# First S5 stage of a four-layer trunk: angle products moved behind the outputs on TensorE, their clips moved on VectorE

## The chip, the cores and the metric

The kernel runs on one core of a Trainium2 chip. A core has a matrix engine (TensorE, PE in the profile; its weight loads are PEld), a vector engine (DVE), a scalar engine (ACT), GpSimd (POOL) and a queue engine (SP) that here only issues DMAs. Each engine takes its own list of instructions strictly in order and waits on semaphores for the others. The metric is the device time of one execution in microseconds; the time before is the median of three runs.

## The reference, cut to what matters

The reference is a trunk of four layers over 512 tokens of width 1024 in fp32: an S5 mixer, a gated linear attention, a differential attention and again an S5 mixer, each followed by a SwiGLU network. The change lies in the first S5 mixer. Its state is complex and diagonal; the powers of the diagonal are needed as magnitudes and as cosines and sines of angles:

```python
ab_mag = jnp.exp(lr * dt)
ab_ang = li * dt
...
p_mag = jnp.exp(lr * dt * j)
p_ang = li * dt * j
p_re = p_mag * jnp.cos(p_ang)
p_im = p_mag * jnp.sin(p_ang)
...
y = jnp.einsum('bcgp,ghp->bcgh', s_re, cr) - jnp.einsum('bcgp,ghp->bcgh', s_im, ci)
...
y = y + d_skip.astype(f32) * h.astype(f32)
z = jax.nn.gelu(y).astype(h.dtype)
a, b = jnp.split(z @ w_glu, 2, axis=-1)
return a * jax.nn.sigmoid(b)
```

The mixer's 64 groups times 64 states are worked through in eight blocks of 512 columns (four state tiles of 128 rows by 128 positions; four tokens are folded into one position).

## The kernel before, in words

`s5_first` runs the first S5 mixer through `s5_pipe`, a loop over ten steps `kk` in which block `kk` has its states made, block `kk - 1` its outputs, and block `kk - 2` its share of the GLU product. The order of instructions on every engine is the order in which this Python code issues them: `hand_all()` switches the automatic scheduler off for the stage, and `s5_first` hangs its own pieces of work into the loop by named hooks (`first`, `behind states`, `operators`, `ahead of zp`, `behind products`, `behind scans`, `beside`). A hook is called at one place of the step, and whatever it issues stands there in the lists of all engines. Behind the stage the scheduler works again.

One step of the loop, in order: hook `first`; six DVE operations that turn the products `V` back by cosine and sine (`states`, L1383 to L1388); hook `behind states`; the outputs of the block before, on PE (`outputs`, tile `y`, L1412 and L1414, then the gelu on ACT, L1416); hook `operators`; the transposition of the inputs two blocks ahead (`up`, L1357, copied by ACT, L1370); hook `ahead of zp`; the transposition of the gelu's result (`zp`, L1429, copied by ACT, L1430); the products `V` of the next block (L1378); hook `behind products`; two scans on DVE (L1392); hook `behind scans`; four multiplications on DVE that turn the scanned states forward (`turn`, L1401 and L1405, into `prods`); hook `beside`; the low half of the gelu's result on DVE (`rest`, L1434); the GLU products (L370 to L372).

The angles of a block come in four pieces (`s5_phases_first`):

- `rough` (L1003, L1004): two PE products over 12 rows give the number of turns, and ACT rounds it in two operations (`turns` L1005, `turnsr` L1007).
- `angle` (L1011 to L1013): three PE products into one PSUM bank; the second takes the whole turns off and so waits for `turnsr`.
- `clip` (L1016): one DVE operation from that bank into the block's table `cs`.
- `sines` (L1019 to L1021): three ACT operations in `cs`. Sine and gelu need different function tables, so ACT loads a table when it changes between them.

`rough` and `angle` take their banks from one group of four (tag `acc`), which the GLU uses later; a bank comes free when its reader (ACT for `rough`, DVE for `angle`) is done. `y`, `up`, `zp`, `xps`, `cps` and `rps` share two banks (tag `tp`).

Other pieces that stand near the change: `new_q` (PE `cps` L1089, ACT copies L1110) and the two halves of `Q` on DVE (L1043 to L1045) make the output operators of two blocks; `out_pads` copies them into place by DMA (`scr<-Q`, L1135, SP's queue). `s5_rows` (PE `rps`, L1145) and `s5_map` make the direct map of two blocks: DVE (L1155) and ACT (L1159) write `rsb`, a DMA takes it to DRAM (`rd<-rsb`, L1161), and eight DMAs, four each on SP and POOL, bring it back in another shape (`scr<-rd`, L1170). The outputs read that map. `ins` makes the input operators (PE `xps` L1179, ACT L1202). `decays` copies the decay on ACT (L1029), and POOL clears its first columns (L1030). Weights of the GLU are split into high and low halves (ACT L346, DVE L350).

Of the kernel before, what the change touches and what calls it, by code (L numbers as in the profile page):

```python
# [268 lines left out]
class Trunk:  # L269
# [1257 lines left out]
    def s5_first(self, ctx):  # L1527
# [5 lines left out]
        with self.tc.tile_pool(name="s5_0", bufs=1) as p:  # L1533
# [24 lines left out]
            def new_x(h):  # L1558
                X[h] = self.s5_x(nc.vector, p, 0, 8 * h, 8, raw[h][0], 2, gain)
                X[h][1]()  # L1560

            def new_q(h):
                Q[h] = self.s5_q(nc.vector, p, 0, 8 * h, 8, 2)
                Q[h][1](self.s5_qt(raw[h][1]))
# [27 lines left out]
            def phases(*pieces):  # L1592
                for kk, name in pieces:
                    if name == "rough":
                        ph[kk] = self.s5_phases_first(kk, cs(kk))
                    ph[kk][name]()

            def decays(kk):
                r4[kk] = p.tile([P, 512], F32, tag="r4", name="r4", bufs=2)
                self.s5_decays(0, kk, r4[kk][:])  # L1600

            def ins(kk):
                self.s5_inms(inm[kk % 2], self.s5_xts(X[kk // 2][0], 4 * (kk % 2)))

            def out_pads(kk):
                self.s5_out_pads(oms[kk % 2], Q[kk // 2][0], slice(4 * (kk % 2), 4 * (kk % 2) + 4))
# [19 lines left out]
                raw[2] = self.s5_loads(p, 0, 16, 8, 2)  # L1626

            def first(kk):
                if kk == 1:
                    phases((5, "angle"))  # L1630
                if kk == 2:
                    raw[3] = self.s5_loads(p, 0, 24, 8, 2)
                if 1 <= kk < 7:
                    decays(kk + 1)

            def behind_states(kk):
                if kk == 0:
                    phases((1, "clip"))
                    self.s5_map(0, 0, 8, rv[0], rs, mops[0])

            def operators(kk):
                if kk in (2, 4, 6):
                    h = kk // 2
                    rv[h] = self.s5_rows(8, bp, Q[h][0])
                    if h > 1:
                        self.s5_map(0, 8 * h, 8, rv[h], rs, mops[h % 2])
                if 1 <= kk < 7:
                    ins(kk + 1)
# [5 lines left out]
            def behind_products(kk):  # L1654
                if kk == 0:
                    phases((3, "angle"), (4, "rough"))
                if kk == 1:
                    phases((6, "rough"), (7, "rough"), (6, "angle"))
                if kk == 2:
                    phases((7, "angle"))  # L1660
                if kk == 3:
                    phases((4, "sines"), (5, "sines"), (6, "sines"), (7, "sines"))
                if kk % 2 == 0 and 2 <= kk < 7:
                    out_pads(kk + 1)

            def behind_scans(kk):
                if kk == 0:
                    phases((2, "clip"), (2, "sines"), (4, "angle"), (5, "rough"))
                if kk == 1:
                    phases((4, "clip"), (5, "clip"))  # L1670
                if kk == 2:
                    self.s5_map(0, 8, 8, rv[1], rs, mops[1])
                    phases((6, "clip"))

            def beside(kk):
                h = kk // 2
                if kk == 2:
                    phases((7, "clip"))
                if kk % 2 == 0 and kk < 6:
                    if kk:  # L1680
                        new_x(h + 1)
                        X[h + 1][2]()
                    X[h + 1][3]()
                    self.s5_b_pads(bp, X[h + 1][0])
                if kk % 2 == 0 and kk < 6:
                    new_q(h + 1)
                if kk == 0:
                    phases((3, "clip"), (3, "sines"))
                if kk % 2 and kk < 7:
                    Q[h + 1][2]()  # L1690
                    Q[h + 1][3]()
                    out_pads(kk + 1)

            rv = {}
            hooks = {
                "first": first, "operators": operators, "behind states": behind_states, "ahead of zp": ahead_of_zp,
                "behind products": behind_products, "behind scans": behind_scans, "beside": beside,
            }
            accs = self.s5_pipe(0, hu, zT, True, room, get, before, hooks)
# [726 lines left out]
```

## Time and profile before

| | before |
|---|---|
| median of three runs | 2325.21 us (2324.91 to 2325.57) |
| profiled execution | 2320.61 us, span 2318.9 us |
| granted TensorE clock, mean | 0.989 |
| PE busy | 2221.3 us, 96% of the span |
| DVE busy | 1593.3 us, 69% |
| ACT busy | 1112.6 us, 48% |
| POOL busy | 284.5 us, 12% |

A row of the timeline has the start and the length in us, the engine, the line of the kernel, the operation, the tile written and the tiles read, and in brackets the idle time of the engine before it with what ended it. SPq is a DMA issue on SP's queue; its length is that of issuing, not of the transfer. A row of a window has the stretch, its length, the busy time of PE, PEld, DVE, ACT and POOL with the number of instructions, then the granted clock of TensorE (1.00 is full speed), the busy share of the DMA engines and GB/s.

### The profile page before, as it was taken

The page shows a single profiled execution, that of the slowest core. Times are in us where ns is not written, and L with a number is a line of the kernel's source. Part 1 is how long each engine was busy: PE and PEld are TensorE (multiplying, and loading weights), DVE is VectorE, ACT ScalarE, POOL GpSimd, SP SyncE. Part 2 cuts the span into 40 slices and gives each one's busy share as a digit, 9 for nine tenths or more (in the row PEclk, how much of TensorE's full clock was granted, in tenths as well). Part 3 has the DMA queues.
Part 4 walks back from the last instruction along what each step waited for, and adds up shares of the span by engine and source line. Part 5 has one row for each costly group of instructions (what it writes and reads, how often), then busy time and mean ns, then how long its engine had stood idle before and what let it go on. Part 6 is the DMA issues. An engine that isn't in the chain of part 4 may idle for free. (4 is left out here: it accounts for less than half of the span.)

```text
span 2318.9 us, 37158 instructions
## 1 busy us (share of the span) xinstructions
PE 2221.3 (96%) x14847; PEld 1969.5 (85%) x14847; DVE 1593.3 (69%) x2461; ACT 1112.6 (48%) x1769; POOL 284.5 (12%) x394
## 2 busy tenths in 40 slices
PE   5899999999999999999999999999999899999997
PEld 3788979898877789898988887899999788989996
DVE  8784877786624578776744675976766965967674
ACT  5533645454453355555535675654534224635342
POOL 1000141522000010101002131110000100101000
PEclk8999999999999999999999999999999999999999
DMA  4156567663422457575336365876641555766531
GB/s 85 37 141 171 138 166 183 169 175 97 129 73 73 133 138 196 155 191 156 100 124 151 91 150 143 216 206 152 171 96 46 140 158 151 191 161 161 160 81 64
DMA packets 293927, 319.91 MB, mean 138 GB/s; under 512 B 70077, under 2 KB 233177, under 8 KB 293498
## 3 DMA queue, kind: packets, MB, share of 16 engines
q1 hardware_dynamic: 231130, 235.79, 33.9%
q0 software_dynamic: 62624, 81.75, 19.1%
q8 instruction: 117, 1.92, 0.3%
q14 instruction: 56, 0.46, 0.1%
HBM read 285.62 MB, written 16.65 MB: 130 GB/s over the span
## 5 line engine op out<-in xcount | busy, mean ns | idle before, releaser
L350 DVE TENSOR_TENSOR whl<-wst,whl 128x1024 fp32r<-128x1024 f32 x272 | 331.9, 1223 | 280.6 <-ACT whl L346 279.8
L346 ACT CAST whl<-wst 128x1024 fp32r<-128x1024 f32 x272 | 285.6, 1052 | 382.8 <-PE acc L372 259.8
L535 PE MATMUL a<-side,whl 128*128 128x256 f32 x3168 | 384.9, 278 | 10.0 <-ACT whl L346 5.9
L535 PEld LDWEIGHTS a<-side,whl 128*128 128x128 f32 x3168 | 371.7, 189 | 12.5 <-ACT whl L346 7.2
L370 PE MATMUL acc<-whl,act 128*128 128x512 f32 x704 | 278.0, 395 | 1.2 <-DVE g L580 0.8
L371 PE MATMUL acc<-whl,act 128*128 128x512 f32 x704 | 274.9, 391 | 0.0
L372 PE MATMUL acc<-whl,act 128*128 128x512 f32 x704 | 274.7, 390 | 0.0
L535 PE MATMUL c<-side,whl 128*128 128x256 f32 x2112 | 255.6, 277 | 5.8 <-DVE whl L350 5.8
L535 PEld LDWEIGHTS c<-side,whl 128*128 128x128 f32 x2112 | 248.1, 189 | 6.6 <-DVE whl L350 6.6
L350 DVE TENSOR_TENSOR whl<-slot,whl 128x1024 fp32r<-128x1024 f32 x105 | 127.9, 1223 | 65.7 <-ACT whl L346 65.1
L370 PEld LDWEIGHTS acc<-whl,act 128*128 128x128 f32 x704 | 132.1, 188 | 30.8 <-DVE g L580 1.2
L372 PEld LDWEIGHTS acc<-whl,act 128*128 128x128 f32 x704 | 132.2, 188 | 27.8
L371 PEld LDWEIGHTS acc<-whl,act 128*128 128x128 f32 x704 | 132.2, 188 | 26.0 <-issue 0.2
L346 ACT CAST whl<-slot 128x1024 fp32r<-128x1024 f32 x105 | 110.1, 1054 | 73.9 <-PE acc L372 28.1
L370 PE MATMUL acc<-whl,hT 128*128 128x512 f32 x352 | 142.9, 406 | 2.1 <-DVE ro L2151 1.5
L371 PE MATMUL acc<-whl,hT 128*128 128x512 f32 x352 | 137.9, 392 | 1.0 <-DVE whl L350 1.0
L372 PE MATMUL acc<-whl,hT 128*128 128x512 f32 x352 | 137.9, 392 | 0.0
L535 PE MATMUL a<-sides,whl 128*128 128x256 f32 x1056 | 134.0, 283 | 1.6 <-DVE x L518 1.6
L535 PE MATMUL d<-sides,whl 128*128 128x256 f32 x1056 | 133.4, 283 | 1.3 <-ACT whl L346 1.3
L535 PEld LDWEIGHTS a<-sides,whl 128*128 128x128 f32 x1056 | 129.5, 191 | 2.7 <-issue 2.0
L535 PEld LDWEIGHTS d<-sides,whl 128*128 128x128 f32 x1056 | 128.9, 191 | 1.9 <-ACT whl L346 1.9
L571 POOL DMA_DIRECT2D wst<-in_ffn_w_gate_up_dram x44 | 57.1, 1297 | 436.5 <-DMA wst<-in_ffn_w_gate_up_dram 239.1
(449 smaller groups left out, 3909.1 us busy)
## 6 DMA issues: line engine op xcount, KB each, us to landing
wst<-in_ffn_w_gate_up_dram SPq DMA_DIRECT2D x88, 512.0 KB, 4.7
wst<-in_ffn_w_down_dram SPq DMA_DIRECT2D x88, 512.0 KB, 4.5
slot<-in_ffn_w_gate_up_dram SPq DMA_DIRECT2D x69, 512.0 KB, 5.5
wst<-in_ffn_w_gate_up_dram POOLq DMA_DIRECT2D x44, 512.0 KB, 6.2
halves<-in_ffn_w_gate_up_dram SPq DMA_DIRECT2D x42, 512.0 KB, 5.7
wst<-in_s_w_glu_dram SPq DMA_DIRECT2D x32, 512.0 KB, 4.5
wst<-in_gla_w_in_dram SPq DMA_DIRECT2D x24, 512.0 KB, 3.7
wst<-in_diff_w_qkv_dram SPq DMA_DIRECT2D x24, 512.0 KB, 3.7
```

The lines of the kernel that those rows point to most:

```text
L346: self.last["high"] = self.nc.scalar.copy(hl[:, 0], w[:])
L350: self.last["low"] = self.nc.vector.tensor_tensor(hl[:, 1], w[:], hl[:, 0].bitcast(F32), op=ALU.subtract)
L370: mm(out, lh, rh, start=first, stop=False)
L371: mm(out, lh, rl, start=False, stop=False)
L372: self.last["mm"] = mm(out, ll, rh, start=False, stop=last)
L535: mm(o, hl[:, x, k, c], side[:, y, k], start=first and not (j or k or n), stop=k == 3 and n == 2, skip_group_check=True,)
L571: nc.gpsimd.dma_start(w[:], left.quarter(*plus, b), accum_op=ALU.add)
```

## The change

Only the places of `angle`, `clip` and `sines` of blocks 3 to 7 in the hooks of the first S5 stage differ. No instruction is added or removed.

- Angle 4 was issued behind the scans of step 0, and angle 5 at the start of step 1. Both now stand in `operators` of step 1, behind the outputs of block 0 on PE.
- Angle 6 stood behind the products of step 1 (ahead of the outputs of block 1), and angle 7 behind the products of step 2. Both now stand in `operators` of step 2, behind the outputs of block 1 and ahead of `s5_rows`.
- Clip 3 and sines 3 were in `beside` of step 0. They are now in `behind states` of step 1: on DVE behind the six operations of step 1's states, on ACT behind the decay of block 2.
- Clips 4 and 5 were behind the scans of step 1. They are now in `beside` of step 1, behind the four turns and ahead of `Q`.
- Clips 6 and 7 and sines 4 to 7 stay where they are.

In the built program PE's list differs by these moves of three products each, DVE's by the three clips, ACT's by one swap (the decay copy of block 2 ahead of sines 3), and SP's list is the same; on POOL two clears of decays are in the same places and write other buffers.

```diff
--- before.py
+++ after.py
@@ -1626,8 +1626,6 @@
                 raw[2] = self.s5_loads(p, 0, 16, 8, 2)
 
             def first(kk):
-                if kk == 1:
-                    phases((5, "angle"))
                 if kk == 2:
                     raw[3] = self.s5_loads(p, 0, 24, 8, 2)
                 if 1 <= kk < 7:
@@ -1637,8 +1635,14 @@
                 if kk == 0:
                     phases((1, "clip"))
                     self.s5_map(0, 0, 8, rv[0], rs, mops[0])
+                if kk == 1:
+                    phases((3, "clip"), (3, "sines"))
 
             def operators(kk):
+                if kk == 1:
+                    phases((4, "angle"), (5, "angle"))
+                if kk == 2:
+                    phases((6, "angle"), (7, "angle"))
                 if kk in (2, 4, 6):
                     h = kk // 2
                     rv[h] = self.s5_rows(8, bp, Q[h][0])
@@ -1655,9 +1659,7 @@
                 if kk == 0:
                     phases((3, "angle"), (4, "rough"))
                 if kk == 1:
-                    phases((6, "rough"), (7, "rough"), (6, "angle"))
-                if kk == 2:
-                    phases((7, "angle"))
+                    phases((6, "rough"), (7, "rough"))
                 if kk == 3:
                     phases((4, "sines"), (5, "sines"), (6, "sines"), (7, "sines"))
                 if kk % 2 == 0 and 2 <= kk < 7:
@@ -1665,9 +1667,7 @@
 
             def behind_scans(kk):
                 if kk == 0:
-                    phases((2, "clip"), (2, "sines"), (4, "angle"), (5, "rough"))
-                if kk == 1:
-                    phases((4, "clip"), (5, "clip"))
+                    phases((2, "clip"), (2, "sines"), (5, "rough"))
                 if kk == 2:
                     self.s5_map(0, 8, 8, rv[1], rs, mops[1])
                     phases((6, "clip"))
@@ -1684,8 +1684,8 @@
                     self.s5_b_pads(bp, X[h + 1][0])
                 if kk % 2 == 0 and kk < 6:
                     new_q(h + 1)
-                if kk == 0:
-                    phases((3, "clip"), (3, "sines"))
+                if kk == 1:
+                    phases((4, "clip"), (5, "clip"))
                 if kk % 2 and kk < 7:
                     Q[h + 1][2]()
                     Q[h + 1][3]()
```

## Prediction

> **What bounds the kernel now.** The page comes first: one core, TensorE (PE) busy nearly throughout, so only stretches in which PE waits or runs at a low clock can give time back.
>
> ```profile
> span 2318.9 us, 37158 instructions
> PE 2221.3 (96%) x14847; PEld 1969.5 (85%) x14847; DVE 1593.3 (69%) x2461; ACT 1112.6 (48%) x1769; POOL 284.5 (12%) x394
> ```
>
> The edit lies in steps 0 to 2 of the first S5 stage. Second, the PE timeline of that place. The reader is to see two waits for ACT's `turnsr`, each ahead of outputs (`y`) that need no angle, and one wait for a DMA.
>
> ```profile
> 51.72 0.62 PE L1003 MATMUL rough<-counts,frow 12*128 12x512 f32 x1
> 52.57 0.62 PE L1011 MATMUL angle<-counts,frow 12*128 12x512 f32 x1
> 54.30 0.79 PE L1012 MATMUL angle<-turnsr,nident 128*128 128x512 f32 x1 [1.11 <-ACT turnsr L1007]
> 55.62 0.62 PE L1003 MATMUL rough<-counts,frow 12*128 12x512 f32 x1
> 58.51 0.79 PE L1011 MATMUL angle<-counts,frow 12*128 12x512 f32 x1
> 60.67 0.80 PE L1412 MATMUL y<-scr,room 128*128 128x128 f32 x2
> 62.97 0.63 PE L1412 MATMUL y<-scr,room 128*128 128x128 f32 x2
> 66.08 0.39 PE L1412 MATMUL y<-scr,room 128*128 128x128 f32 x2
> 67.29 1.15 PE L1179 MATMUL xps<-ident,X 64*64 64x64 f32 x32
> 74.34 0.49 PE L1012 MATMUL angle<-turnsr,nident 128*128 128x512 f32 x1 [0.84 <-ACT turnsr L1007]
> 81.43 0.69 PE L1145 MATMUL rps<-Q,bpad 128*32 128x64 f32 x32
> 82.19 1.15 PE L1179 MATMUL xps<-ident,X 64*64 64x64 f32 x32
> 88.32 0.50 PE L1011 MATMUL angle<-counts,frow 12*128 12x512 f32 x1
> 89.59 1.09 PE L1089 MATMUL cps<-ident,craw 128*64 128x128 f32 x16
> 94.47 0.46 PE L1412 MATMUL y<-scr,room 128*128 128x128 f32 x2 [0.84 <-DMA scr<-rd]
> 99.10 1.15 PE L1179 MATMUL xps<-ident,X 64*64 64x64 f32 x32
> 115.14 1.30 PE L1179 MATMUL xps<-ident,X 64*64 64x64 f32 x32 [3.32 <-ACT z L1416]
> ```
>
> Third, the same place in windows (busy time of PE, PEld, DVE, ACT, POOL, then granted clock). The clock changes at multiples of 3.41 us: half speed from 44.32 to 64.80 (six stretches) and again at 75.04 and at 116.00 (one each).
>
> ```profile
> 44.32:61.39 17.07, 15.96 (x52) 10.29 (x52) 13.20 (x21) 11.14 (x22) 2.46 (x5) 0.50 0.31 62
> 61.39:64.80 3.41, 3.41 (x18) 3.41 (x17) 3.41 (x7) 2.09 (x3) 0.11 (x1) 0.50 0.00 0
> 64.80:68.21 3.41, 3.41 (x53) 3.29 (x53) 2.86 (x5) 0.60 (x1) 0.00 (x0) 1.00 0.00 0
> 71.63:75.04 3.41, 2.57 (x12) 1.53 (x10) 3.41 (x6) 2.13 (x4) 0.00 (x0) 1.00 0.37 58
> 75.04:78.45 3.41, 3.41 (x16) 3.19 (x16) 3.00 (x4) 2.03 (x3) 0.10 (x1) 0.50 0.02 5
> 81.87:85.28 3.41, 2.06 (x53) 1.52 (x43) 3.05 (x7) 1.43 (x3) 0.00 (x0) 1.00 0.37 77
> 112.59:116.00 3.41, 0.86 (x28) 0.86 (x30) 3.41 (x6) 2.60 (x5) 0.11 (x1) 1.00 0.00 0
> 116.00:119.41 3.41, 3.17 (x22) 2.66 (x19) 3.41 (x6) 2.29 (x4) 1.76 (x4) 0.50 0.32 72
> 115.14:170.10 54.96, 50.97 (x452) 45.39 (x452) 47.26 (x72) 19.38 (x30) 5.19 (x11) 0.97 0.47 129
> ```
>
> What decides here is the clock. One block of outputs takes 62.97 − 60.67 = 2.30 us slow and 67.29 − 66.08 = 1.21 (with the step to `xps`) fast, so a slow stretch of 3.41 us full of work costs about half of it, 1.71. The stretch that brought the clock back, 61.39 to 64.80, holds outputs alone. What went before it mixed in `rough` and `angle`, products over 12 of 128 rows. The stretch of `rough` and `angle` at 71.63 cost the clock again. I read this as: 12-row products count for little, outputs for full.
>
> **The change, part by part.** *Angles 4 and 5 behind the first outputs.* PE's order becomes rough 4, rough 5, `cps`, outputs 0, angles 4 and 5. Ahead of the outputs go 55.62 − 52.57 = 3.05 us (angle 4 with its wait) and 60.67 − 58.51 = 2.16 (angle 5), so outputs 0 start at 60.67 − 5.21 = 55.46, if their map is there by then. Its DMAs are these:
>
> ```profile
> 46.41 1.76 SPq L1170 DMA_DIRECT2D scr<-rd  x4
> 46.70 2.35 POOL L1170 DMA_DIRECT2D scr<-rd  x4 [2.13 <-DMA rd<-rsb]
> ```
>
> Two steps later the same DMAs, issued from 89.66 on (below), let PE go at 94.47, 4.81 us after; from 46.70 that gives 51.5, four before they are needed. The angles' own work is done later, so 1.11 of the 3.05, the wait, is gain by itself.
>
> *Angles 6 and 7 behind the second outputs.* The wait of 0.84 goes. Angle 7, 89.59 − 88.32 = 1.27, moves from behind the products of step 3 to ahead of `rps` (81.43), where more hangs on it.
>
> *What hangs on `rps`.* It feeds a map that goes through DVE, ACT and two DMAs before outputs 2 may start:
>
> ```profile
> 87.51 0.30 ACT L1159 COPY rsb<-rps 128x96 f32<-128x96 f32 x1
> 87.83 0.37 SPq L1161 DMA_DIRECT2D rd<-rsb  x1
> 89.66 2.99 SPq L1170 DMA_DIRECT2D scr<-rd  x4
> ```
>
> That is 94.47 − 81.43 = 13.04 us, all behind `rps`, and PE waits at its end. So outputs 2 move by what `rps` moves, no more. The 1.27 taken from between them is no gain there. From outputs 2, ACT's chain (copy, sines 4 to 7, gelu) leads to `xps` at 115.14, and PE is then busy 50.97 of 54.96 us: the shift passes on to the end of the stage. Behind it the instruction order is unchanged, and I let the shift pass in full.
>
> *Sum without the clock:* −1.11 − 0.84 + 1.27 = −0.68.
>
> *The clock.* Outputs 0 at half speed from 55.46 fill all of 57.97 to 61.39 and 2.51 of the 3.41 us before it, the rest of which is `cps` (64 columns, no 12-row product). The trace has no stretch of just that mix. From the one that returned on outputs alone, the return is at 61.39 at the latest, one slow stretch less (−1.71); if `cps` counts, at 57.97, two less (−3.41). I take two, since 116.00 to 119.41, made of `xps`, `up` and `zp` beside products, also brought the clock back. The second slow stretch should go: roughs 6 and 7 are followed at once by outputs 1, and the 0.84 of idling is gone (−1.71; other bound 0). The third, after 3.32 us of idling that stays, I keep (bound −1.71). Clock: −5.12.
>
> *Clips on DVE and their cover.*
>
> ```profile
> 51.95 0.69 DVE L1016 TENSOR_SCALAR cs<-angle 128x512 f32<-128x512 f32 x1 [2.13 <-PE angle L1013]
> 60.78 0.69 DVE L1016 TENSOR_SCALAR cs<-angle 128x512 f32<-128x512 f32 x1 [1.71 <-PE angle L1013]
> 63.78 0.68 DVE L1043 TENSOR_TENSOR Q<-Q,pw 128x512 f32<-128x512 f32 x1
> 67.03 0.69 DVE L1045 TENSOR_TENSOR Q<-Q,dq 128x512 f32<-128x512 f32 x1
> 89.69 0.69 DVE L1016 TENSOR_SCALAR cs<-angle 128x512 f32<-128x512 f32 x1 [4.11 <-PE angle L1013]
> ```
>
> Clip 3 goes behind the states of step 1, so its 2.13 vanishes. Clips 4 and 5 now wait for angles behind outputs 0, and `Q` is queued behind them: outputs 0 end near 61.4 (55.46 + 2.30 + 3 × 1.21), two angles at 1.27 each end near 63.9, a clip takes 0.69, and `Q` (63.78 to 67.72, 3.94 long) ends near 68.5 in place of 67.7. Its first reader is `rps`, near 76 then, so it costs nothing; at a slow clock `Q` ends near 71, still covered. Without that cover it would cost up to 3.5. Clip 7's 4.11 goes as angle 7 moves up, and everything DVE does behind 89.69 can start earlier; that is needed, as otherwise DVE would hold the gain back.
>
> *ACT, SP, POOL.*
>
> ```profile
> 61.59 0.60 ACT L1029 COPY r<-s5r 128x512 f32<-128x512 f32 x1
> 62.21 1.28 ACT L1416 ACT_TABLE_LOAD   x1
> ```
>
> The decay copy passes the three sines of block 3, and POOL's memset follows it: the same work in another order, done by 62.21 + 1.28 = 63.49 at the latest. Gelu 0, whose outputs end near 61.4, can thus be 2.1 late; PE has two angles (2.54) and `xps` (1.15) between, which hide it. If they did not, 2.1 is the price. No DMA is reordered on SP or POOL; bounds 0 and 0.84, the longest DMA wait above.
>
> **Sum:** −0.68 − 5.12 = −5.80 against the profiled execution's 2320.61 (span 2318.9 and 1.7 around it): 2314.8. The runs' median is 2325.21, 4.6 above it, so the forecast is 2319.4.
>
> **Rivals.** *The clock returns when it does now.* Only −0.68 remains, or −2.4 with one stretch less: 2324.5 to 2322.8. For it: five of the six stretches after 44.32 held much PE work and stayed slow. Against it: none of those held outputs alone. [...]
>
> *Slower: the clock falls later and stays down.* Angles 6 and 7, `rps`, the narrow `xps`, and the wait for ACT before `up` come in one piece behind outputs 1. For it: that piece looks like 71.63 to 75.04. Against: 81.87 to 85.28 holds most of it, 2.06 busy, and stayed fast. [...] Three more slow stretches (5.1) eat up the clock's gain; from four on it is slower.
>
> *More than forecast:* the third stretch goes too: −7.5, 2317.7.
>
> **How the numbers follow.** 0.2% is 4.65 us, about what a measurement of this kernel can tell from no change. Forecast 0.47, more 0.13: both below 2320.6, faster 0.60. Clock as now, or one stretch: 0.25, same. Slower 0.15. The gate's 3.41 us grid can fall otherwise by one stretch either way, and idle stretches later in the kernel can catch or miss one (1.71 each): so the low end is two stretches under the case of more, 2317.7 − 3.42 = 2314.3, and the high end, leaving out the slower rival, is the median less 0.68 and one stretch more, 2326.2. The forecast's own range is 2317.5 to 2321.
>
> **What would show it.** Outputs 0 near 55.5; granted clock 1.00 from 58 or 61.4, and none at half between 71 and 82; no wait of `angle` for `turnsr`; clip 7 on DVE without its 4.11; outputs 2 near 89 and the `xps` behind gelu near 109. Wrong: 0.50 from 78 on, a PE wait for `Q` at `rps`, or the shift gone by 170.

## The result and the profile after

The changed kernel takes 2318.88 us (median of seven executions, 2312.34 to 2323.66) against 2325.67 us before (seven, 2324.91 to 2332.58): a ratio of 0.9964, with a 95% interval of 0.9951 to 0.9977, some 8.4 us. The ratios here are not quotients of the medians, which lie 6.8 us apart. The forecast was 2319.4.

The profiled execution after took 2318.88 us, its span 2317.2. That is only 1.7 us less than the profiled span before (2318.9), because most of what this profile wins in the stage of the change is lost again behind it. The timeline of TensorE (PE) after, in the stage of the change:

```profile
55.07 0.80 PE L1412 MATMUL y<-scr,room 128*128 128x128 f32 x2
57.37 0.51 PE L1412 MATMUL y<-scr,room 128*128 128x128 f32 x2
58.60 0.39 PE L1412 MATMUL y<-scr,room 128*128 128x128 f32 x2
60.93 0.50 PE L1011 MATMUL angle<-counts,frow 12*128 12x512 f32 x1
61.36 0.49 PE L1012 MATMUL angle<-turnsr,nident 128*128 128x512 f32 x1
69.20 0.49 PE L1412 MATMUL y<-scr,room 128*128 128x128 f32 x2
76.23 0.69 PE L1145 MATMUL rps<-Q,bpad 128*32 128x64 f32 x32
79.28 0.66 PE L1357 MATMUL up<-ident,scr 128*128 128x128 f32 x4 [1.27 <-ACT inm L1202]
88.81 0.46 PE L1412 MATMUL y<-scr,room 128*128 128x128 f32 x2 [0.20 <-issue]
109.46 1.97 PE L1179 MATMUL xps<-ident,X 64*64 64x64 f32 x32 [3.30 <-ACT z L1416]
```

Outputs 0, 1 and 2 start at 55.07, 69.20 and 88.81 (before: 60.67, 75.26, 94.47), each some 6 us sooner. Of the 5.60 at outputs 0, 0.38 was there before anything that was moved: `rough` of block 3 starts at 44.60, against 44.98. Angles 4 and 5 no longer wait for `turnsr`. The first quarter of outputs 0 still takes 2.30 us, the second 1.23: the clock came back at 57.60, just behind the start of the second. The windows of the same trace show the clock (PE, PEld, DVE, ACT, POOL busy, then the granted clock):

```profile
43.95:57.60 13.65, 13.65 (x55) 10.46 (x55) 13.62 (x22) 8.93 (x18) 2.46 (x5) 0.50 0.36 78
57.60:81.50 23.90, 21.27 (x218) 17.00 (x218) 18.26 (x30) 14.23 (x23) 0.21 (x2) 1.00 0.19 34
78.09:81.50 3.41, 1.55 (x12) 1.31 (x13) 3.34 (x7) 1.91 (x4) 0.00 (x0) 1.00 0.00 0
81.50:84.91 3.41, 3.41 (x20) 3.19 (x21) 3.31 (x10) 0.96 (x2) 0.32 (x1) 0.50 0.14 38
105.40:108.81 3.41, 0.76 (x34) 0.53 (x32) 1.80 (x4) 3.38 (x5) 0.10 (x1) 1.00 0.00 0
108.81:115.64 6.83, 5.94 (x50) 5.42 (x51) 6.73 (x15) 3.56 (x6) 2.09 (x4) 0.50 0.35 76
170.00:2300.00 2130.00, 2083.30 (x13706) 1856.58 (x13705) 1442.19 (x2133) 1019.87 (x1619) 264.43 (x346) 0.99 0.54 142
272.64:276.05 3.41, 3.37 (x16) 3.37 (x17) 3.41 (x5) 1.78 (x2) 1.32 (x1) 0.50 0.65 208
```

The long half-speed stretch has become four stretches of 3.41 us, from six. The second did not go away: it moved from 75.04 to 81.50, behind 3.41 us in which PE was busy 1.55. The third became two stretches. The first gate of the GLU on ACT (L1780), which stands at the end of the stage, shows what is left of it all. The row of before, then that of after:

```profile
170.37 2.05 ACT L1780 ACTIVATE gate<-acc 128x512 f32<-128x512 f32 x4
```

```profile
165.25 2.05 ACT L1780 ACTIVATE gate<-acc 128x512 f32<-128x512 f32 x4
```

The stage is 5.12 us shorter, the 0.38 included. Behind it, where the lists of instructions are the same, the profiled execution after was at half speed for 27.30 us, the one before for 17.06. The window from 170 to 2300 shows it as a granted clock of 0.99, against 1.00 before:

```profile
170.00:2300.00 2130.00, 2082.56 (x13717) 1854.92 (x13716) 1443.93 (x2133) 1024.66 (x1625) 264.82 (x346) 1.00 0.55 143
272.64:276.05 3.41, 1.97 (x18) 1.77 (x16) 3.03 (x3) 0.93 (x2) 0.00 (x0) 1.00 0.80 230
```

One of the additional stretches is 272.64 to 276.05, fast before and slow after. On ACT, where the same operations can be set side by side, the lead falls from 5.15 to 3.93 us there and is 1.72 at the end: 3.4 of the 5.12 us are lost again in this pair. That these stretches took them is read from where the lead falls; no run holds them fixed. Over all executions the gain stands.

### The profile page after: what moved, and what is told of

The parts are those of the page before. It is cut to its first block, busy times and chain, and to the rows that moved or that the text cites. A ratio compares the mean times of both kernels' runs of the same rounds, so it can differ in the third digit from the quotient of the medians.

```text
span 2317.2 us, 37158 instructions
## 1 busy us (share of the span) xinstructions
PE 2223.4 (96%) x14847; PEld 1972.9 (85%) x14847; DVE 1593.3 (69%) x2461; ACT 1111.1 (48%) x1769; POOL 284.4 (12%) x394
```

## Experiments

Two theories run through the expectations. One says that the gain is the clock's: products over 12 of 128 rows count for little in what the clock goes by, outputs for full (Theory C). The rival (Theory O) says that it is the order's: waits and work taken off the path by the moves themselves. Each experiment is told with its profile's first gate, and with the half-speed time in the stage.

### Each half of the change alone

The first kernel moves angles 4 and 5 with their clips, and leaves block 3's clip and angles 6 and 7 as they were:

```diff
             def first(kk):
-                if kk == 1:
-                    phases((5, "angle"))
...
             def operators(kk):
+                if kk == 1:
+                    phases((4, "angle"), (5, "angle"))
...
-                    phases((2, "clip"), (2, "sines"), (4, "angle"), (5, "rough"))
-                if kk == 1:
-                    phases((4, "clip"), (5, "clip"))
+                    phases((2, "clip"), (2, "sines"), (5, "rough"))
...
                     phases((3, "clip"), (3, "sines"))
+                if kk == 1:
+                    phases((4, "clip"), (5, "clip"))
```

> Only angles 4 and 5 (with their clips) move; angle 6 stays ahead of the outputs of block 1, angle 7 behind the products, clip 3 in its old place. Stage end read at the first GLU gate on ACT (L1780; 170.4 us before, 165.3 after). Theory C (the gain is mostly the TensorE clock coming back sooner): outputs 0 start near 55, the clock is back at 1.00 by 58 to 61.4 in place of 64.8, gate at 165.5 to 167.5, total 2.5 to 5 us under before. Theory O (the gain is the waits that go, the clock only accompanies): outputs 0 start near 55 too, but the gate comes 1.1 us sooner than before (169.3), total 1.1 under.

The second moves angles 6 and 7 alone:

```diff
             def operators(kk):
+                if kk == 2:
+                    phases((6, "angle"), (7, "angle"))
...
-                    phases((6, "rough"), (7, "rough"), (6, "angle"))
-                if kk == 2:
-                    phases((7, "angle"))
+                    phases((6, "rough"), (7, "rough"))
```

> Only angles 6 and 7 move behind the outputs of block 1. Theory C: outputs 0 at 60.7 and the clock back at 64.8 as before, the half-speed stretch at 75.0 to 78.5 gone, rps at 81.43 + 1.27 - 0.84 - 1.71 = 80.2, gate near 169.1, total about 1.3 us under before; if a stretch of half speed comes behind 78 in its place, no gain or 0.4 slower. Theory O: rps at 81.9, gate 0.4 us later than before (170.8).

Angles 4 and 5 alone: 2325.97 us against 2330.01 before on the same chip, ratio 0.9973 (0.9959 to 0.9987), about −6.3 us. Angles 6 and 7 alone: 2326.37, ratio 0.9990 (0.9977 to 1.0003), about −2.3 us and not told from nothing. The two add up to the whole, −8.6 against −8.4. The ratios put the larger part on angles 4 and 5, but their intervals overlap and the two medians lie 0.4 us apart, so this isn't shown. The PE timeline with angles 4 and 5 moved:

```profile
55.38 0.80 PE L1412 MATMUL y<-scr,room 128*128 128x128 f32 x2
70.42 0.50 PE L1012 MATMUL angle<-turnsr,nident 128*128 128x512 f32 x1 [0.84 <-ACT turnsr L1007]
90.67 0.46 PE L1412 MATMUL y<-scr,room 128*128 128x128 f32 x2 [0.95 <-DMA scr<-rd]
```

Outputs 0 start where they start in the whole change, the clock is back at 57.41 (half speed from 43.76 for 13.65 us), and the wait of angle 6 for `turnsr` is still there, followed by a half-speed stretch at 71.07. The gate comes at 166.19, with 20.48 us at half speed. With angles 6 and 7 alone the gate came at 166.16, with 27.31 us at half speed, but that profile says little on its edit. The clock was fast there from 48.24 to 51.65 and outputs 0 started at 57.46 (60.7 was expected), ahead of anything that the edit touches. The same list of instructions can thus meet the clock in different ways, which is why the next runs change the clock's cause itself.

### The same order with products over 128 rows

If products over 12 rows keep the clock low, they should not when all 128 rows are driven. This edit gives the operands of `rough` and `angle` 128 rows, of which rows 12 to 127 are zeros. The products have the same values, and PE has the same number of instructions; POOL gets two more, which clear the tiles. The edit was made in the kernel before and in the changed kernel:

```diff
-        self.frow = cp.tile([12, 8, P], F32R, name="frow")
+        self.frow = cp.tile([P, 8, P], F32R, name="frow"); nc.gpsimd.memset(self.frow[:].bitcast(F32), 0.0)
...
-        self.counts = cp.tile([12, 2, 4, P], F32R, name="counts")
+        self.counts = cp.tile([P, 2, 4, P], F32R, name="counts"); nc.gpsimd.memset(self.counts[:].bitcast(F32), 0.0)
...
-                self.counts[:, z], y[:12].unsqueeze(2).broadcast_to([12, 4, P]),
+                self.counts[:12, z], y[:12].unsqueeze(2).broadcast_to([12, 4, P]),
...
-            nc.scalar.copy(self.frow[:, 4 * q : 4 * q + 4], ps[:12])
+            nc.scalar.copy(self.frow[:12, 4 * q : 4 * q + 4], ps[:12])
```

> The kernel before, with the two 12-row operands of rough and angle widened to 128 rows, rows 12 to 127 zero: same instructions, same values, 128 rows of TensorE in use where 12 were. Theory C in my reading (12-row products count for little towards the clock): the half-speed time between 44 and 79 us shrinks from 23.9 to under 12, gate at 160 to 166, total 4 to 10 us under before, with no change of order at all. If the clock counts the time that products stream and not their rows, or if rows of zeros don't count: half speed from 44.3 to 64.8 and at 75 as before, gate within 1 us of 170.4. Theory O: total unchanged whatever the clock does.

> The changed kernel with the same 128-row operands. If the widening lifts the clock in both, what is left between this and the widened kernel before is the order alone: -0.7 us (waits of 1.11 and 0.84 gone, angle 7 of 1.27 ahead of rps), gate 0.5 to 1.5 sooner than with the order of before. If the order itself is worth the gain (Theory O): 5 us sooner. If the widening does nothing: gate at 165.3 as after.

Both were run a second time on another chip:

> Second look at the order of before with the clock mostly up. Over the looks so far the gate is 153.9 + 0.55 us per us of half speed in the stage; by that 153.9 plus its own slow time, plus 1 to 2 for the order of before. Gate 157 to 163; ratio 0.993 to 0.997.

> Second look at the changed order with the clock mostly up. Theory C: at equal slow time in the stage 0.7 to 1.6 us ahead of e10, outputs 1 about 3 ahead, outputs 2 about 0.7 to 1.7 ahead, the total not to be told from e10. Theory O: gate 5 us ahead of e10 at equal slow time.

| | first time | second time | first gate, us |
|---|---|---|---|
| order of before, 128 rows | 0.9945 (0.9925 to 0.9965) | 0.9950 (0.9933 to 0.9966) | 161.25, 155.73 |
| changed order, 128 rows | 0.9949 (0.9933 to 0.9965) | 0.9950 (0.9933 to 0.9967) | 161.51, 156.06 |

The order of before with 128 rows gains some 12 us, by the ratios more than the change itself, though the intervals overlap. With it the change adds nothing that the totals can tell, and the lead of 0.5 to 1.5 us that was expected at the gate did not come. The gate of the second order of before, 155.73, is earlier than expected (157 to 163). The windows of the second time, order of before:

```profile
40.00:72.00 32.00, 26.27 (x268) 22.49 (x267) 31.90 (x51) 24.20 (x41) 2.67 (x7) 1.00 0.34 65
72.00:107.00 35.00, 28.61 (x283) 25.31 (x282) 32.15 (x58) 21.52 (x35) 4.41 (x10) 0.95 0.23 48
```

and those of the changed order:

```profile
40.00:72.00 32.00, 26.81 (x276) 23.33 (x275) 31.90 (x51) 24.71 (x41) 2.69 (x7) 1.00 0.34 64
72.00:107.00 35.00, 30.36 (x278) 27.41 (x277) 33.33 (x61) 20.92 (x34) 4.40 (x10) 0.85 0.26 53
```

From 40 to 72 the granted clock is 1.00 in both, and in the first pair too, where before it was 0.50 from 44.32 to 64.80. PE is busy a smaller share of the time (26.3 of 32 us, against 15.96 of 17.07 at half speed before), so a larger busy share is not what keeps the clock up. A part of the lead is older than 40 us. The record of the granted clock has its first entry, 1.00, at 37.49 in the kernel before and at 31.73 here; ahead of it the windows print 1.00, but products have their half-speed length. The first product of block 0's `angle` (L1011) takes 0.79 us at 31.14 in the kernel before and 0.50 at 31.95 here.

The edit changed one thing more than the rows, which its expectations had not seen. In the profile after, at a granted clock of 1.00, a 12-row `angle` takes from 60.93 to the next instruction at 62.12, 1.19 us: the three products start 0.43 and 0.42 apart. With 128 rows it is 0.78. The order of before with 128 rows, PE timeline:

```profile
45.10 0.48 PE L1011 MATMUL angle<-counts,frow 128*128 128x512 f32 x1
45.42 0.39 PE L1012 MATMUL angle<-turnsr,nident 128*128 128x512 f32 x1
45.65 0.39 PE L1013 MATMUL angle<-counts,frow 128*128 128x512 f32 x1
45.88 0.40 PE L1003 MATMUL rough<-counts,frow 128*128 128x512 f32 x1
```

From the start of each product to the next start that is 0.43, 0.42 and 0.34 us against 0.32, 0.23 and 0.23, so 0.11, 0.19 and 0.11 more. The author's estimate from these steps is that a change between products of few rows and of 128 cost PE 0.1 to 0.2 us here. For the six angles from 40 us on that is an estimated 6 × 0.41 = 2.5 us of the 12 at most that are not the clock's; part of it turns into longer waits (1.49 us for `turnsr` at 48.23, against 1.11 before). The gaps themselves may also be what keeps the clock low.

The pair of the second time also shows what the order does with 128 rows. PE timeline, order of before with 128 rows:

```profile
51.93 0.39 PE L1412 MATMUL y<-scr,room 128*128 128x128 f32 x2
63.92 0.38 PE L1412 MATMUL y<-scr,room 128*128 128x128 f32 x2
81.25 0.46 PE L1412 MATMUL y<-scr,room 128*128 128x128 f32 x2 [1.11 <-DMA scr<-rd]
101.93 1.15 PE L1179 MATMUL xps<-ident,X 64*64 64x64 f32 x32 [3.34 <-ACT z L1416]
```

and the changed order with 128 rows:

```profile
49.58 0.46 PE L1412 MATMUL y<-scr,room 128*128 128x128 f32 x2 [1.69 <-DMA scr<-rd]
61.23 0.38 PE L1412 MATMUL y<-scr,room 128*128 128x128 f32 x2
79.96 0.46 PE L1412 MATMUL y<-scr,room 128*128 128x128 f32 x2 [0.40 <-issue]
100.62 1.97 PE L1179 MATMUL xps<-ident,X 64*64 64x64 f32 x32 [3.31 <-ACT z L1416]
```

The changed order starts outputs 1 by 2.69 us and outputs 2 by 1.29 us sooner (3.08 and 1.73 in the first pair). The lead is still there at the `xps` behind them, which then runs at half speed and takes 1.97 instead of 1.15: this execution had two stretches at 99.83, the other one at 103.41. At the gate the lead is gone (156.06 against 155.73).

### The same with 64 rows

To separate rows from gaps, the operands in the order of before got 64 rows, of which 12 to 63 are zeros:

```diff
-        self.frow = cp.tile([12, 8, P], F32R, name="frow")
+        self.frow = cp.tile([64, 8, P], F32R, name="frow"); nc.gpsimd.memset(self.frow[:].bitcast(F32), 0.0)
...
-        self.counts = cp.tile([12, 2, 4, P], F32R, name="counts")
+        self.counts = cp.tile([64, 2, 4, P], F32R, name="counts"); nc.gpsimd.memset(self.counts[:].bitcast(F32), 0.0)
```

> The operands of rough and angle in the order of before get 64 rows, of which rows 12 to 63 are zeros. It is to separate two things that 128 rows changed together. At a granted clock of 1.00 one block's angle takes 1.19 us from its first product to the next instruction with 12 rows (60.93 to 62.12 in the profile after), and 0.78 with 128 rows (45.10 to 45.88): each change between products of few rows and of 128 costs 0.1 to 0.2 us. So PE had small gaps as well as few rows. If the gaps at each change of rows keep the clock low, they stay with 64 rows (1.19 again) and half speed stays from about 44 to 65: outputs 0 near 60.7, ratio 1.000, first gate 170 to 173. If the rows that are driven count (Theory C), five times as many should bring the clock back sooner though the gaps are there: granted clock over 0.75 from 44 to 65, outputs 0 between 53 and 57, ratio 0.995 to 0.998, first gate 160 to 166. If the angle takes 0.78 with 64 rows as well, gaps and rows stay unseparated.

Ratio 0.9988 (0.9978 to 0.9998), which is 2.8 us, about a quarter of what 128 rows gave; the medians, 2326.21 against 2327.20, are 1.0 apart. The gaps stayed, as an `angle` at full clock takes 1.20 here (41.22 to 42.42 on PE). The half-speed stretch stayed too, but for one stretch in the middle:

```profile
44.76:65.24 20.48, 19.18 (x73) 13.91 (x74) 17.74 (x28) 13.40 (x24) 2.58 (x6) 0.58 0.26 52
51.59:55.00 3.41, 2.11 (x7) 1.14 (x7) 2.68 (x5) 2.15 (x4) 0.00 (x0) 1.00 0.71 149
55.00:65.24 10.24, 10.24 (x46) 7.87 (x46) 9.41 (x15) 7.19 (x13) 0.11 (x1) 0.50 0.03 10
```

Outputs 0 start at 60.13 and the gate comes at 171.70, as the expectation had it for the gaps; 0.58 in place of 0.50 is far from the 0.75 expected for the rows. So 64 rows do little for the stage. Whether 128 rows help because the array is full, or because the changes of rows and their gaps are gone, the totals and the gates don't separate; one stretch, told behind the next runs, speaks for the rows. What they show is that the clock was low here with the mixture of few-row and 128-row products (0.50 from 44.32 to 64.80 with 12 rows, 0.58 from 44.76 to 65.24 with 64), and not with 128 rows in all of them (1.00 from 40 to 72).

### Both kernels once more

> The kernel before, unchanged, for a second profile and for the size of what differs from one execution to the next. If the half-speed stretches are set by the order of the work, those of the first S5 stage come back within one stretch of 3.41 us (half speed from 41 to 44 on until 61 to 65, again near 72 to 78), gate (L1780) between 166 and 171; the stretches behind 200 us fall elsewhere and move the total by several us. If they are chance in the stage too, the gate falls anywhere between 160 and 172.

> The changed kernel, unchanged, for a second profile. Theory C: outputs 0 near 55, clock back by 57 to 61.4, gate 163.5 to 167, 3 to 6 us ahead of this call's before. Total over the rounds 4 to 10 us under before (ratio 0.9957 to 0.998). If the first result owed something to its chip or its moment: ratio within 0.002 of 1.

The kernel before against itself: 0.9998 (0.9987 to 1.0009). The changed kernel: 0.9977 (0.9963 to 0.9990), 2322.51 against 2327.59, which is 5.4 us by the ratio and 5.1 by the medians. The new profile of before has the same long half-speed stretch, from 47.40 to 64.47, and 34.13 us at half speed in the stage. The new profile of after has half speed for one stretch at 46.39 and three at 73.69, 17.07 us in all:

```profile
46.39:49.80 3.41, 3.41 (x15) 2.81 (x14) 3.38 (x8) 2.76 (x5) 2.35 (x4) 0.50 0.38 64
49.80:73.69 23.89, 23.04 (x213) 18.09 (x214) 22.47 (x33) 17.22 (x28) 0.21 (x2) 1.00 0.34 64
73.69:83.93 10.24, 8.30 (x66) 7.49 (x64) 10.04 (x23) 2.91 (x5) 1.11 (x3) 0.50 0.08 18
```

The gates are at 173.21 and 162.66, both outside what was expected (166 to 171, 163.5 to 167). The long stretch is shorter in both profiles of after; the later stretch, three times as long here, is the "falls later and stays down" of the prediction's slower rival. It did not outweigh the gain.

The clock came back at 49.80 here, and did not at 50.81 in the new profile of before. One product stands differently in the stretches ahead of these times. The first row is of the new profile of after, the other two of the new profile of before:

```profile
49.14 0.79 PE L1011 MATMUL angle<-counts,frow 12*128 12x512 f32 x1
49.79 0.79 PE L1011 MATMUL angle<-counts,frow 12*128 12x512 f32 x1
50.51 0.80 PE L1012 MATMUL angle<-turnsr,nident 128*128 128x512 f32 x1
```

In the stretch of after, which ends at 49.80, products over 12 rows hold PE for 0.66 us. In that of before, from 47.40 to 50.81, they hold it for 0.72, and the clock stayed low. The first profiles of before and after have eleven stretches of 3.41 us at half speed, from 44 to 85 us, in which PE is busy throughout. In the four that ended in full speed these products (from the start of each to that of the next) hold at most 0.22 us, in the seven that did not at least 0.74. So one list of PE instructions met the clock in two ways, with stretches that began at 46.39 and at 47.40; that the 12-row products decided it is the author's reading. With 64 rows the same `angle` held 0.72 us of the stretch from 48.17 to 51.59, with the same changes of rows, and the clock came back. That speaks for the number of rows rather than the gaps, by one stretch. It tells nothing of when the clock falls: 3.41 us with PE busy 2.06 kept it up before (81.87 to 85.28), and 2.57 did not.

### The clip of block 3 alone

```diff
+                if kk == 1:
+                    phases((3, "clip"), (3, "sines"))
...
-                if kk == 0:
-                    phases((3, "clip"), (3, "sines"))
```

> Only clip 3 and sines 3 move behind the states of step 1; TensorE's list is that of the kernel before. DVE's wait of 2.13 before clip 3 goes, the states of step 1 start near 50 in place of 52.6. Theory C: nothing follows, since outputs 0 stand on TensorE where they stood: outputs 0 at 60.7, clock back at 64.8, gate within one stretch's worth (1.7) of before, ratio within 0.0015 of 1. Theory O, with DVE as the bound: gate 2 us sooner, total 2 us under.

Ratio 0.9997 (0.9984 to 1.0011). On DVE the states of step 1 start at 50.75 and clip 3 follows at 54.34, without its wait of 2.13 us, yet outputs 0 start at 60.53 as before (60.67, 60.78). The move of clip 3 brings nothing by itself. Clips 4 and 5 moved with their angles only and were not run alone.

### The map ahead of outputs 2

The prediction had outputs 2 hang on `rps` through a chain of ACT, DMA and DMA. The copy of the map on ACT (L1159) stood behind the scans' hook. Here it comes at once behind `s5_rows`, in the changed kernel, and, for the second of these kernels, in the changed kernel with 128 rows:

```diff
-    def s5_map(self, L, b0, nb, rv, rs, dst, compact=False):
+    def s5_map(self, L, b0, nb, rv, rs, dst, compact=False, copied=False):
...
-        nc.scalar.copy(rs[:, :nk, 64:112], rv[:, :nk, 16:64])
+        None if copied else nc.scalar.copy(rs[:, :nk, 64:112], rv[:, :nk, 16:64])
...
-                    rv[h] = self.s5_rows(8, bp, Q[h][0])
+                    rv[h] = self.s5_rows(8, bp, Q[h][0]); h == 1 and nc.scalar.copy(rs[:, :2, 64:112], rv[1][:, :2, 16:64])
...
-                    self.s5_map(0, 8, 8, rv[1], rs, mops[1])
+                    self.s5_map(0, 8, 8, rv[1], rs, mops[1], copied=True)
```

> The changed kernel with ACT's copy of the second map (L1159) issued right behind rps in place of behind the copy of zp, so it need not wait for that copy. The step tested: outputs 2 hang on rps by 12.6 to 13.0 us. If so the DMA starts near 77.8 in place of 82.6, the map lands 5 us sooner, outputs 2 follow the GLU products with no wait, near 87.6 in place of 88.8 (with the clock as in the first profile of after), and the gate comes about 1.2 sooner. If the chain is not what holds outputs 2: 88.8 as before.

> The changed kernel with both edits that helped: 128-row operands and the early copy of the map. If both gains are independent: no half speed before 70, outputs 2 follow the GLU products without a wait, gate 157 to 160 (161.5 less 1.2 to 3.2), total 9 to 14 us under before, ratio 0.994 to 0.996 or better. If both remove the same time (a clock that is up already leaves nothing for the map to gain): gate at 161 to 162 and the ratio of e4 and e8, 0.995.

The first gives 0.9949 (0.9933 to 0.9964), 2318.59, where the changed kernel gave 0.9977 on the same chip; the intervals just touch, and the first result of the changed kernel was 0.9964. Its timeline on PE, ACT and SP's queue:

```profile
76.12 0.69 PE L1145 MATMUL rps<-Q,bpad 128*32 128x64 f32 x32
77.82 0.65 PE L1357 MATMUL up<-ident,scr 128*128 128x128 f32 x4
79.66 1.95 PE L1378 MATMUL V<-room,inm 128*128 128x128 f32 x16
85.55 0.46 PE L1412 MATMUL y<-scr,room 128*128 128x128 f32 x2
76.92 0.24 ACT L1648 COPY rsb<-rps 128x96 f32<-128x96 f32 x1 [2.46 <-PE rps L1145]
77.63 0.37 SPq L1161 DMA_DIRECT2D rd<-rsb  x1
```

The issue to DRAM goes out at 77.63 instead of 82.49, and outputs 2 start 9.43 us behind `rps` instead of 12.58, with no wait. How much of these 3.1 us is the chain's is not shown, since in the profile of the changed kernel PE worked until 0.20 us ahead of outputs 2. PE itself is ahead here: `up` starts at 77.82 without its wait of 1.27 (79.28 in the changed kernel), and the products `V` take 1.95 us at full speed, where there they ran in the half-speed stretch from 81.50:

```profile
81.10 3.25 PE L1378 MATMUL V<-room,inm 128*128 128x128 f32 x16
```

That this profile had no half speed between 57.33 and 105.11 may come of that missing wait or of where its stretches fell. That the chain holds outputs 2 once the clock is up, two rows of the kernels with 128 rows show, the changed order (first time) and the same with the early copy:

```profile
81.74 0.77 PE L1412 MATMUL y<-scr,room 128*128 128x128 f32 x2 [3.70 <-DMA scr<-rd]
77.61 0.46 PE L1412 MATMUL y<-scr,room 128*128 128x128 f32 x2 [0.16 <-issue]
```

Outputs 2 start 14.50 us behind `rps` in the one and 10.53 in the other. With 128 rows as well: 0.9944 (0.9926 to 0.9963), 2315.44 against 2327.89, gate at 153.45, the earliest of all (157 to 160 was expected). Its total is not to be told from the two kernels with 128 rows without it (0.9950).

## Why the prediction was right

The forecast, 2319.4, was met by 2318.88. To half a microsecond that is luck: seven executions spread from 2312.34 to 2323.66, the second measurement gave 2322.51, and two of its terms were off in opposite directions. The mechanism that it named, the clock coming back sooner, is seen in every profile in which angles 4 and 5 moved and the products had 12 rows; by the estimate below the clock is half of the gain or somewhat more, and not nearly all of it. Its steps:

- **Outputs 0 at 55.46.** 55.07 in the profile after (55.45 without its head start of 0.38) and 55.38 with angles 4 and 5 alone, 52.66 where the clock came back earlier still. Right.
- **Return two stretches sooner, at 57.97, not one.** 57.60, 57.41 and 57.33 in three profiles, 49.80 in a fourth, there ahead of outputs 0; with the order of before up to there 64.80, 64.47, 64.15 and 61.89. Right. The step rested on reading `cps` as full work; the profiles agree with it, though none tests `cps` alone.
- **12-row products count for little.** That the clock was low with them and not with 128 rows is shown (0.50 from 44.32 to 64.80, against 1.00 from 40 to 72). That it is for the number of their rows is not shown: 64 rows changed little in the stage, and the gaps at each change of rows are a candidate too. One stretch (0.72 us of 64-row products, and the clock came back) speaks for the rows.
- **The second slow stretch should go (−1.71).** This step failed. It went from its place (57.60 to 81.50 is fast), but one stretch came at 81.50, and three at 73.69 in the second profile. Angles 6 and 7, `rps`, the narrow `xps` and the wait of 1.27 for ACT follow one another, and PE was busy 1.55 of the 3.41 us ahead of 81.50. The prediction had this as its slower rival; it came at one stretch and at three. In the kernel with the early map, where the wait of 1.27 was gone, it did not come.
- **The third stretch is kept.** It stayed behind the wait for gelu (3.30), at two stretches in the first profile of after and one in the second; the two profiles of before had one and two. It changes between executions of one kernel.
- **Order alone −0.68.** (Angle 7 stood behind the products of step 2, not of step 3 as the sum says; its 1.27 is the same.) Under-sized, as far as the runs tell: outputs 2 come 1.3 to 1.7 us sooner in the pairs with 128 rows. There the waits for `turnsr` that the moves take off are longer, too (1.49, 0.49 and 0.85 in the second order of before, where the sum had 1.11 and 0.84). That outputs 2 move by what `rps` moves was right (1.31 and 1.29 in the second pair). That they hang on the chain was right where PE waits for it (0.84 before, 3.70 with 128 rows); in the profile after PE's own work filled the 12.58 us but for 0.20.
- **Clips and DMAs at nothing.** The run with clip 3 alone agrees (0.9997); clips 4 and 5 have no run. At the low clock no DMA wait shows at outputs 0; with 128 rows they wait 1.69 for the map.

How much is the clock's and how much the order's can only be estimated. The two pairs of profiles differ: at the prediction's price, half of the slow time, 3.42 us less at half speed are worth 1.71 of the 5.12 at the gate in the first, and 17.06 us less 8.5 of 10.55 in the second. The four profiles with the PE order of before and 12 or 64 rows (clip 3 alone among them) have 27.31, 34.13, 30.72 and 30.72 us at half speed in the stage, 30.72 on average, and the two of after (23.89, 17.07) 20.48. Their gates fit 159.76 us + 0.40 for each us at half speed − 3.95 (standard error 0.8) for the change, which gives 10.24 × 0.40 = 4.1 us to the clock and 4.0 to the order. With the four profiles of the 128-row kernels as well, the fit is 154.46 + 0.57 − 2.37 (standard error 0.8): 5.8 and 2.4. Both add up to 8.1 or 8.2, against the 8.4 of the ratio. The first fit has six profiles for three unknowns, so its 4.1 and 4.0 are each uncertain by some 2 us; neither counts the half speed ahead of the clock's first entry, and the totals of the 128-row pairs show nothing of the order. The prediction had 5.12 and 0.68. By these fits the clock's term was about right; the order's was mis-sized, at 2.4 to 4.0, and made up for what the clock lost in the second and third stretch. Where the order gains more than the 1.3 to 1.7 us seen at outputs 2 is not settled.

The rival "the clock returns when it does now" fell with the return at 57.60. PE's busy time alone does not tell in these traces when the clock changes: before, it stayed at 0.50 through 15.96 busy us of 17.07 (44.32 to 61.39) and at 1.00 behind a stretch with PE busy 2.06 of 3.41 (81.87 to 85.28), and it fell behind stretches with PE busy 2.57 (before) and 1.55 and 0.76 (after).

Open are what the clock goes by, above all when it falls, and why the stretches in the rest of the kernel fall otherwise from one execution to the next. These made the profiled pair differ by 1.7 us only.

## What to carry to other kernels

Look at the granted clock stretch by stretch before looking at waits: here a stage ran at 0.50 for 20.48 us with TensorE busy for 19.37 of them, and the order and the shape of its products changed that (0.50 for 13.65 us from 43.95 with the new order, 1.00 from 40 to 72 with 128 rows). Where products over few rows alternate with products over all rows, widening them with zeros to the full 128 is cheap to try, and here gained more than the reordering (0.9945 and 0.9950, against 0.9964 and 0.9977). Do not read a gain of a few us from one pair of profiles: where half-speed stretches fall differently, compare the stage, and take the total from many executions.

## What the hardware showed that was not expected

- An `angle` took 1.19 us with 12 rows, 1.20 with 64, 0.78 with 128, at a granted clock of 1.00; by the estimate above a change between products of few rows and of 128 cost PE 0.1 to 0.2 us.
- With operands of 128 rows, 116 of them zeros, the granted clock was 1.00 from 40 to 72, where with 12 rows it was 0.50 from 44.32 to 64.80; with 64 rows it was 0.58 from 44.76 to 65.24.
- Of eleven half-speed stretches with PE busy throughout, in the first profiles of before and after, the four with at most 0.22 us of 12-row products in their 3.41 us ended in full speed, the seven with 0.74 or more did not. In the second profiles one with 0.66 did and one with 0.72 did not.
- The clock changed at multiples of 3.41 us within a profile, but not at the same times in each. The long stretch of the same kernel began at 44.32 and at 47.40, 3.08 apart, with 27.31 and 34.13 us at half speed in the stage; the changed kernel had 23.89 and 17.07.
